# Splitting three output stores of a matmul kernel unevenly over queues and partitions

## The chip, the cores and the metric

The kernel runs on one core of one Trainium2 chip. The metric is the device time of one execution in microseconds (us), as the median of several runs. The core has TensorE for matrix products, VectorE, ScalarE and GpSimd for element work, SyncE for issuing transfers, and 16 DMA engines that move data between device memory (DRAM) and the on-chip memory SBUF, whose 128 rows are called partitions. A DMA is issued by one engine's queue; its data are spread over DMA engines, and each of these adds one step to a semaphore when its share has landed. A full count is 16.

## What is computed

```python
def setup_inputs():
    batch, m, k, n = 16, 512, 1024, 768
    return {
        "x": np.random.randn(batch, m, k).astype(np.float32),
        "weight": np.random.randn(k, n).astype(np.float32),
        "sub_value": np.random.randn(batch, m, n).astype(np.float32),
    }

def reference(x, weight, sub_value):
    return (np.matmul(x, weight) - sub_value).astype(np.float32)
```

The 16 x 512 rows are taken as one matrix of 8192 rows, cut into 64 "m tiles" of 128 rows. `x` has 33.6 MB, `weight` 3.1 MB, `sub_value` and the output 25.2 MB each: 87 MB in all.

## The kernel before

Everything that goes to or from DRAM is issued by SyncE in one fixed order. In the list, `x` is a load of x, `w` one of the weights, `s` one of sub_value, and `o` a store of the output; the numbers are the first m tile and how many.

```python
SEGMENTS = [(at, 8) for at in range(0, 64, 8)]
NX, NSO = 16, 32
TRANSFERS = [
    ('x', 0, 1), ('w', 0, 1), ('x', 1, 1), ('w', 1, 1), ('x', 2, 1), ('w', 2, 1),
    # ... cut ...
    ('o', 8, 8), ('o', 16, 8), ('s', 40, 8), ('x', 48, 8), ('s', 48, 8), ('x', 56, 8),
    ('o', 24, 8), ('o', 32, 8), ('s', 56, 8), ('o', 40, 8), ('o', 48, 8), ('o', 56, 5),
    ('o', 61, 2), ('o', 63, 1),
]
```

The m tiles of one segment (8 of them, 1024 rows) are interleaved over the partitions, so that partition p holds rows 8p to 8p+7 of the segment. A transfer of n m tiles is then, for each partition, one contiguous piece of DRAM of n x 3072 bytes (n x 4096 for x):

```python
    def view(flat, at, n):
        first, size = next(one for one in SEGMENTS if one[0] <= at < sum(one))
        assert at + n <= first + size
        rows = flat[first * P : (first + size) * P].rearrange("(p j) c -> p j c", p=P, j=size)
        return rows[:, at - first : at - first + n]
```

sub_value is loaded into a ring of 32 slots, `so_ring`. The result is written over it in place and stored from there. A store waits for the subtraction of its last m tile (`finish`), a load of sub_value for the store that frees its slots:

```python
            need, by = {
                "w": (set(), "o"),
                "x": ({t for t in old if t >= 0}, "cast"),
                "s": ({t for t in old if t >= 0}, "o"),
                "o": (span, "finish"),
            }[kind]
            # ... cut ...
            here = ring[:, at % size : at % size + n]
            there = view(flat, at, n)
            # ... cut: waits ...
            sem, value = lane((kind, at))
            for t in span:
                landed[kind, t] = (sem, value)
                {"x": of_x, "s": of_s, "o": of_o}[kind][t] = (kind, at)
            if kind == "o":
                here, there = there, here
            sp.add(lambda here=here, there=there: nc.sync.dma_start(out=here, in_=there), waits, (sem, 16))
```

ScalarE rounds x to half precision (`cast`), TensorE (or, for some m tiles, VectorE) transposes it, and TensorE multiplies it with the resident weights; for each m tile there are 8 steps along k, each with two halves of 384 columns. VectorE subtracts:

```python
    def finish(mi):
        assert mi in done["s"]
        done["finish"].add(mi)
        o = so_ring[:, mi % NSO].rearrange("p (h n) -> p h n", h=2)
        po = po_b[:, slot["po", mi]]
        dve.add(lambda: nc.vector.tensor_tensor(
            out=o, in0=po[:, :, :NS], in1=o, op=mybir.AluOpType.subtract
        ), [landed["s", mi], (counter["mul"], mul_at[mi])], count("finish"))
        finish_at[mi] = so_far["finish"]
        issue()
```

At the end SyncE waits for all semaphores of transfers that nothing has waited for yet, closes the program's section, and waits for the last m tile's store:

```python
    left = [one for one in lanes if not one["tags"] <= known]
    last = next(one for one in left if of_o[n_mt - 1] in one["tags"])
    for one in left:
        if one is not last:
            nc.sync.wait_ge(one["sem"], one["value"])
    section.close()
    with tc.tile_critical(sync_engine=mybir.EngineType.SP, no_gpsimd_drain=True):
        nc.sync.wait_ge(last["sem"], last["value"])
```

GpSimd clears three small buffers near the start and does nothing after that.

Of the kernel before, what the change touches and what calls it, by code (L numbers as in the profile page):

```python
# [8 lines left out]
P = 128  # L9
# [5 lines left out]
NX, NSO = 16, 32  # L15
# [16 lines left out]
    ('s', 4, 4), ('x', 12, 4), ('s', 8, 8), ('x', 16, 2), ('x', 18, 6), ('s', 16, 8),  # L32
    ('x', 24, 8), ('o', 0, 8), ('s', 24, 8), ('x', 32, 8), ('s', 32, 8), ('x', 40, 8),
    ('o', 8, 8), ('o', 16, 8), ('s', 40, 8), ('x', 48, 8), ('s', 48, 8), ('x', 56, 8),
    ('o', 24, 8), ('o', 32, 8), ('s', 56, 8), ('o', 40, 8), ('o', 48, 8), ('o', 56, 5),
    ('o', 61, 2), ('o', 63, 1),
]


class Queue:  # L40
# [65 lines left out]
def kernel(  # L106
# [7 lines left out]
    nc = tc.nc  # L114
# [3 lines left out]
    out_flat = out.flatten_outer_dims()  # L118

    M_TOT, K = x_flat.shape  # L120
    _, N = weight.shape
    n_mt = M_TOT // P
# [5 lines left out]
# [6 lines that stand above are left out]
# [6 lines left out]
    def sbuf(name, shape, dtype):  # L140
        return ctx.enter_context(nc.sbuf_tensor(name, shape, dtype)).ap()
# [11 lines left out]
    so_ring = sbuf("so_ring", [P, NSO, N], F32)  # L153
# [11 lines left out]
    counter = {}  # L165
# [4 lines left out]
    def count(name):  # L170
        so_far[name] += 1
        return (counter[name], 1)

    sp, pe = Queue(nc, nc.sync), Queue(nc, nc.tensor)
    act, dve, pool = Queue(nc, nc.scalar), Queue(nc, nc.vector), Queue(nc, nc.gpsimd)
# [6 lines left out]
        out=along, data0=ones, data1=ones, initial=0.0, op0=mybir.AluOpType.mult, op1=mybir.AluOpType.add,  # L182
    ), waits=[(counter["ident"], 1)], then=count("ident"))
    dve.add(lambda: nc.vector.transpose(across, along), waits=[(counter["ident"], 3)], then=count("ident"))  # L184
    for a in range(P // Q):
        here = slice(a * Q, (a + 1) * Q)
        dve.add(lambda here=here: nc.vector.tensor_tensor(  # L187
            out=ident[here, here], in0=along[here], in1=across[here], op=mybir.AluOpType.is_equal,
# [16 lines left out]
    landed = {}  # L205
    cast_at, evac_at, pair_at, turn_at, mul_at, finish_at, w_at = {}, {}, {}, {}, {}, {}, {}
# [16 lines left out]
    done = {"w": set(), "x": set(), "s": set(), "o": set(), "cast": set(), "finish": set()}  # L223
    staged = {}
    lanes = []
    of_x, of_s, of_o = {}, {}, {}
    known = set()

    def lane(tag):

        for one in lanes:
            if one["tags"] <= known:
                break
        else:
            one = {"sem": tc.alloc_semaphore(f"lane{len(lanes)}"), "value": 0, "tags": set()}
            lanes.append(one)
        one["value"] += 16
        one["tags"].add(tag)
        return one["sem"], one["value"]

    def issue():
        nonlocal known
        while todo:
            kind, at, n = todo[0]
            span = set(range(at, at + n))
            old = {t - NX if kind == "x" else t - NSO for t in span}
            need, by = {
                "w": (set(), "o"),
                "x": ({t for t in old if t >= 0}, "cast"),
                "s": ({t for t in old if t >= 0}, "o"),  # L250
                "o": (span, "finish"),
            }[kind]
            if not need <= done[by]:
                return
            todo.pop(0)
            done[kind] |= span
            if kind == "w":

                first = NSO - 2 * (n_c - at)
                st = so_ring[:, first : first + 2]  # L260
                sem, value = lane((kind, at))
                sp.add(lambda st=st, at=at: nc.sync.dma_start(out=st, in_=w_c[at]), then=(sem, 16))  # L262
                for r in range(2):
                    dve.add(
                        lambda at=at, r=r, st=st: nc.vector.tensor_copy(out=w_sb[:, at, r], in_=st[:, r]),  # L265
                        waits=[(sem, value)], then=count("w"),
                    )
                    staged[first + r] = so_far["w"]
                w_at[at] = so_far["w"]
                continue  # L270
            ring, size, flat = {
                "x": (x_ring, NX, x_flat), "s": (so_ring, NSO, sub_flat), "o": (so_ring, NSO, out_flat)
# [3 lines that stand above are left out]
            waits = []  # L276
            if kind == "x" and need:
                waits.append((counter["cast"], max(cast_at[t] for t in need)))
                last = max(need, key=lambda t: cast_at[t])
                known |= {tag for t, tag in of_x.items() if t in cast_at and cast_at[t] <= cast_at[last]}  # L280
            if kind == "s":
                for t in need:
                    waits.append(landed["o", t])
                    known.add(of_o[t])
                for t in span:
                    if t % NSO in staged:
                        waits.append((counter["w"], staged.pop(t % NSO)))
                        known |= {("w", c) for c in w_at if w_at[c] <= waits[-1][1]}
            if kind == "o":
                waits.append((counter["finish"], max(finish_at[t] for t in need)))  # L290
                known |= {of_s[t] for t in finish_at if finish_at[t] <= max(finish_at[u] for u in need)}
            sem, value = lane((kind, at))
            for t in span:
                landed[kind, t] = (sem, value)
                {"x": of_x, "s": of_s, "o": of_o}[kind][t] = (kind, at)
            if kind == "o":
                here, there = there, here
            sp.add(lambda here=here, there=there: nc.sync.dma_start(out=here, in_=there), waits, (sem, 16))  # L298

    def cast(mi):  # L300
        assert mi in done["x"]
        done["cast"].add(mi)
        x_in = x_ring[:, mi % NX]
        first = mi - mi % 2
        waits = [landed["x", mi]]
        if first in ON_DVE:
            if mi == first:
                b, before = take("x16p", N16P, mi)
                if before is not None:
                    waits.append((counter["pair"], pair_at[before]))  # L310
            to = x16p_b[:, slot["x16p", first], mi - first]
        else:
            b, before = take("x16", N16, mi)
            if before is not None:
                waits.append((counter["turn"], turn_at[before]))
            to = x16_b[:, b]
        act.add(lambda: nc.scalar.copy(out=to, in_=x_in), waits, count("cast"))  # L317
        cast_at[mi] = so_far["cast"]
        issue()
# [92 lines left out]
# [14 lines that stand above are left out]
# [59 lines left out]
    for mi in range(HEAD + (EARLY is not None), n_mt):  # L485
# [3 lines left out]
        t = mi + TA  # L489
# [32 lines left out]
    for one in left:  # L522
        if one is not last:
            nc.sync.wait_ge(one["sem"], one["value"])
    section.close()
    with tc.tile_critical(sync_engine=mybir.EngineType.SP, no_gpsimd_drain=True):
        nc.sync.wait_ge(last["sem"], last["value"])
# [30 lines left out]
```

## Time and profile before

| | us |
|---|---|
| device time, median of 3 runs (lowest to highest) | 210.52 (210.41 to 210.6) |
| span of the profiled run, first to last instruction | 208.6 |
| TensorE busy | 195.2 |
| VectorE busy | 128.2 |
| ScalarE busy | 109.0 |
| GpSimd busy | 1.0 |
| last subtraction starts | 201.68 |
| last store issued | 202.66 |

The span in the profile starts with the first instruction and is a little shorter than the device time. In the profile's lines PE is TensorE, DVE is VectorE, ACT is ScalarE, POOL is GpSimd and SPq is SyncE's sequencer, which issues the transfers. "L198" is a line of the kernel. A row of digits gives the busy share in tenths in 40 equal slices of the stretch that was asked for; "DMA" is the mean over the 16 DMA engines. A row of a transfer ends in its size and the median time from its issue to its landing, that is, to the last of its 16 semaphore steps. q1 is the queue of all transfers of data, and q8 and q14 carry instructions to the engines.

### The profile page before, as it was taken

What the parts mean: (1) busy time and instruction counts of PE and PEld (TensorE: products, weight loads), DVE (VectorE), ACT (ScalarE), POOL (GpSimd) and SP (SyncE); (2) the same over time, 40 slices, a digit from 0 to 9 for tenths busy, and PEclk for the clock granted to TensorE, in tenths of its full rate; (3) what the DMA queues carried; (4) which work ended last, traced back from release to release, by engine and by line L of the source; (5) the groups of instructions that cost most, each with busy time, mean ns of one, the idle gap of its engine ahead of it and who ended that gap; (6) DMA issues with size and microseconds to landing.
All of it is one profiled execution on the core that took longest, in us unless ns stands there. A gap on an engine that the chain in (4) does not pass through costs nothing.

```text
span 208.6 us, 2612 instructions
## 1 busy us (share of the span) xinstructions
PE 195.2 (94%) x1234; PEld 75.5 (36%) x700; DVE 128.2 (61%) x224; ACT 109.0 (52%) x113; POOL 1.0 (0%) x7
## 2 busy tenths in 40 slices
PE   6999799969999999999999999999999999999960
PEld 0233243324434433443443443343344344334410
DVE  2323224975993795598399379469739938952330
ACT  3655759506673761944745576183564737507300
POOL 1000000000000000000000000000000000000000
PEclk9999999999999999999999999999999999999997
DMA  6999999999999999999999999999999999999993
GB/s 204 421 427 434 441 424 434 445 429 424 434 448 452 366 443 424 459 415 418 449 440 424 419 429 443 423 470 393 434 463 401 441 424 429 438 443 419 419 422 135
DMA packets 5476, 87.08 MB, mean 417 GB/s; under 512 B 608, under 2 KB 608, under 8 KB 1888
## 3 DMA queue, kind: packets, MB, share of 16 engines
q1 hardware_dynamic: 5472, 87.03, 97.9%
q8 instruction: 1, 0.02, 0.0%
q14 instruction: 3, 0.02, 0.0%
HBM read 61.87 MB, written 25.17 MB: 417 GB/s over the span
## 4 chain that ended last, share of the span: by engine, by line
PE 75%; DMA 13%; DVE 6%; SPq 3%; issue 1%; DVEq 0%
PE po_b L198 67%; DMA so_ring<-in_sub_value_dram 13%; PE pt_b L335 8%; DVE xtp_b L368 3%; DVE so_ring L417 2%; SPq L298 2%; SPq L262 1%; SPq L553 0%; DVEq L59 0%; SPq L138 0%
## 5 line engine op out<-in xcount | busy, mean ns | idle before, releaser
L198 PE MATMUL po_b<-w_sb,xt_b 128*128 128x384 f16 x704 | 126.0, 326 | 1.2 <-DVE w_sb L265 0.9
L417 DVE TENSOR_TENSOR so_ring<-po_b,so_ring 128x768 f32<-128x768 f32 x64 | 60.8, 957 | 59.3 <-PE po_b L198 39.9
L348 ACT COPY xt_b<-pt_b 128x1024 f16<-128x1024 f16 x44 | 44.5, 1012 | 65.3 <-PE pt_b L335 64.3
L368 DVE STREAM_TRANSPOSE xtp_b<-x16p_b 32x256 f32<-32x256 f32 x144 | 62.7, 435 | 2.3
L198 PE MATMUL po_b<-w_sb,xtp_b 128*128 128x384 f16 x320 | 61.3, 326 | 1.9 <-DVE xtp_b L368 1.7
L397 PEld LDWEIGHTS <-xt_b 128*128 128x128 f16 x352 | 34.4, 98 | 58.9 <-issue 55.6
L317 ACT CAST x_b<-x_ring 128x1024 f16<-128x1024 f32 x46 | 47.2, 1048 | 5.0 <-DMA x_ring<-in_x_dram 4.9
L335 PE MATMUL pt_b<-ident,x_b 128*128 128x128 f32 x184 | 47.5, 274 | 1.7 <-ACT x_b L317 1.7
L335 PEld LDWEIGHTS pt_b<-ident,x_b 128*128 128x128 f32 x184 | 25.4, 141 | 44.6 <-issue 36.8
L317 ACT CAST x16p_b<-x_ring 128x1024 f16<-128x1024 f32 x18 | 18.8, 1046 | 14.9 <-DMA x_ring<-in_x_dram 14.9
L397 PEld LDWEIGHTS <-xtp_b 128*128 128x128 f16 x160 | 15.7, 98 | 20.4 <-issue 18.3
L265 DVE CAST w_sb<-so_ring 128x768 f16<-128x768 f32 x8 | 4.1, 556 | 11.6 <-DMA so_ring<-in_weight_dram 11.6
L198 PE MATMUL po_b<-idle_x,idle_w 128*128 128x512 f16 x26 | 7.7, 448 | 1.7 <-POOL idle_x L178 1.7
L348 ACT COPY xtp_b<-pt_b 128x1024 f16<-128x1024 f16 x2 | 2.0, 1012 | 2.5 <-PE pt_b L335 2.5
L317 ACT ACT_TABLE_LOAD x1 | 1.3, 1283 | 0.9 <-SPq L138 0.9
L427 PEld LDWEIGHTS <-idle_w 128*128 128x128 f16 x4 | 0.4, 99 | 1.7 <-POOL idle_x L178 1.7
L187 DVE TENSOR_TENSOR ident<-along,across 32x32 f32<-32x32 f32 x4 | 0.7, 183 | 0.1
L179 DVE MEMSET ones<- 128x32 f32 x1 | 0.1, 85 | 1.0 <-SPq L138 1.0
L178 POOL MEMSET idle_x<- 128x512 f16 x1 | 0.5, 528 | 0.0
L499 ACT CAST stub<-ident 128x1 f16<-128x1 f32 x2 | 0.4, 194 | 0.0
L184 DVE STREAM_TRANSPOSE across<-along 128x32 f32<-128x32 f32 x1 | 0.2, 212 | 0.0
L476 POOL MEMSET mark<- 128x1 f32 x1 | 0.1, 98 | 23.7 <-ACT xtp_b L348 23.7
(7 smaller groups left out, 1.0 us busy)
## 6 DMA issues: line engine op xcount, KB each, us to landing
so_ring<-in_sub_value_dram SPq DMA_DIRECT2D x7, 3072.0 KB, 24.2
out_dram<-so_ring SPq DMA_DIRECT2D x7, 3072.0 KB, 26.6
x_ring<-in_x_dram SPq DMA_DIRECT2D x5, 4096.0 KB, 23.1
x_ring<-in_x_dram SPq DMA_DIRECT2D x2, 2048.0 KB, 27.2
so_ring<-in_weight_dram SPq DMA_DIRECT2D x4, 768.0 KB, 8.3
x_ring<-in_x_dram SPq DMA_DIRECT2D x1, 3072.0 KB, 28.8
x_ring<-in_x_dram SPq DMA_DIRECT2D x2, 1024.0 KB, 24.8
out_dram<-so_ring SPq DMA_DIRECT2D x1, 1920.0 KB, 10.2
```

What stands on the lines that cost most here:

```text
L178: pool.add(lambda: nc.gpsimd.memset(idle_x, 0.0), then=count("idle"))
L187: dve.add(lambda here=here: nc.vector.tensor_tensor(out=ident[here, here], in0=along[here], in1=across[here], op=mybir.AluOpType.is_equal, ...
L198: return nc.tensor.add_instruction(mybir.InstMatmult(name=nc.get_next_instruction_name(), engine=full.engine, ins=list(full.ins), outs=lis ...
L262: sp.add(lambda st=st, at=at: nc.sync.dma_start(out=st, in_=w_c[at]), then=(sem, 16))
L265: lambda at=at, r=r, st=st: nc.vector.tensor_copy(out=w_sb[:, at, r], in_=st[:, r]),
L298: sp.add(lambda here=here, there=there: nc.sync.dma_start(out=here, in_=there), waits, (sem, 16))
L317: act.add(lambda: nc.scalar.copy(out=to, in_=x_in), waits, count("cast"))
L335: pe.add(lambda: nc.tensor.transpose(words, from_, ident), waits, count("turn") if last else None)
L348: act.add(lambda: nc.scalar.copy(out=to, in_=pt_b[:, b]), waits, count("evac"))
L368: dve.add(lambda: nc.vector.transpose(xt[b * Q : (b + 1) * Q, :, a * Q : (a + 1) * Q], x16[a * Q : (a + 1) * Q, :, b * Q : (b + 1) * Q],), ...
L397: pe.add(lambda weights=weights: nc.tensor.ldweights(weights, tile_position=(0, 0)), [w for w in waits if w[0] in ready])
L417: dve.add(lambda: nc.vector.tensor_tensor(out=o, in0=po[:, :, :NS], in1=o, op=mybir.AluOpType.subtract), [landed["s", mi], (counter["mul"] ...
```

## The change

The store of m tiles 40 to 47 is cut: SyncE stores 40 to 45, and GpSimd's own queue stores 46 and 47, in three transfers of 5, 112 and 11 partitions, once they are computed and the last load of sub_value has landed. The store of m tiles 61 and 62 stays with SyncE but goes out as two transfers, of partitions 0 to 119 and 120 to 127. The same bytes are stored to the same places. [...] the change is a way to give the 16 DMA engines unequal shares of these stores. Each GpSimd transfer has a semaphore of its own, for which SyncE waits at the close.

```diff
--- before.py
+++ after.py
@@ -32,9 +32,11 @@
     ('s', 4, 4), ('x', 12, 4), ('s', 8, 8), ('x', 16, 2), ('x', 18, 6), ('s', 16, 8),
     ('x', 24, 8), ('o', 0, 8), ('s', 24, 8), ('x', 32, 8), ('s', 32, 8), ('x', 40, 8),
     ('o', 8, 8), ('o', 16, 8), ('s', 40, 8), ('x', 48, 8), ('s', 48, 8), ('x', 56, 8),
-    ('o', 24, 8), ('o', 32, 8), ('s', 56, 8), ('o', 40, 8), ('o', 48, 8), ('o', 56, 5),
+    ('o', 24, 8), ('o', 32, 8), ('s', 56, 8), ('o', 40, 6), ('q', 46, 2), ('o', 48, 8), ('o', 56, 5),
     ('o', 61, 2), ('o', 63, 1),
 ]
+OWN = (112, 117), (0, 112), (117, 128)
+SPLIT = {61: ((0, 120), (120, 128))}
 
 
 class Queue:
@@ -225,6 +227,7 @@
     lanes = []
     of_x, of_s, of_o = {}, {}, {}
     known = set()
+    own = []
 
     def lane(tag):
 
@@ -249,11 +252,21 @@
                 "x": ({t for t in old if t >= 0}, "cast"),
                 "s": ({t for t in old if t >= 0}, "o"),
                 "o": (span, "finish"),
+                "q": (span, "finish"),
             }[kind]
             if not need <= done[by]:
                 return
             todo.pop(0)
-            done[kind] |= span
+            done["o" if kind == "q" else kind] |= span
+            if kind == "q":
+                here, there = so_ring[:, at % NSO : at % NSO + n], view(out_flat, at, n)
+                waits = [(counter["finish"], max(finish_at[t] for t in need)), landed["s", n_mt - 1]]
+                for low, high in OWN:
+                    own.append(tc.alloc_semaphore(f"own{low}"))
+                    pool.add(lambda low=low, high=high, here=here, there=there: nc.gpsimd.dma_start(
+                        out=there[low:high], in_=here[low:high], max_dma_last_dim=4 * N,
+                    ), waits, (own[-1], 16))
+                continue
             if kind == "w":
 
                 first = NSO - 2 * (n_c - at)
@@ -289,13 +302,16 @@
             if kind == "o":
                 waits.append((counter["finish"], max(finish_at[t] for t in need)))
                 known |= {of_s[t] for t in finish_at if finish_at[t] <= max(finish_at[u] for u in need)}
-            sem, value = lane((kind, at))
+            if kind == "o":
+                here, there = there, here
+            for low, high in SPLIT.get(at, ((0, P),)) if kind == "o" else ((0, P),):
+                sem, value = lane((kind, at))
+                sp.add(lambda here=here[low:high], there=there[low:high]: nc.sync.dma_start(
+                    out=here, in_=there
+                ), waits, (sem, 16))
             for t in span:
                 landed[kind, t] = (sem, value)
                 {"x": of_x, "s": of_s, "o": of_o}[kind][t] = (kind, at)
-            if kind == "o":
-                here, there = there, here
-            sp.add(lambda here=here, there=there: nc.sync.dma_start(out=here, in_=there), waits, (sem, 16))
 
     def cast(mi):
         assert mi in done["x"]
@@ -522,6 +538,8 @@
     for one in left:
         if one is not last:
             nc.sync.wait_ge(one["sem"], one["value"])
+    for sem in own:
+        nc.sync.wait_ge(sem, 16)
     section.close()
     with tc.tile_critical(sync_engine=mybir.EngineType.SP, no_gpsimd_drain=True):
         nc.sync.wait_ge(last["sem"], last["value"])
```

## The prediction

> **What bounds the kernel now.** I read three views in this order. First the page's top: busy shares, slices and DMA queues.
>
> ```profile
> PE 195.2 (94%) x1234; PEld 75.5 (36%) x700; DVE 128.2 (61%) x224; ACT 109.0 (52%) x113; POOL 1.0 (0%) x7
> ...
> DMA  6999999999999999999999999999999999999993
> ...
> q1 hardware_dynamic: 5472, 87.03, 97.9%
> ```
>
> Two resources are full: TensorE at 94%, and the 16 DMA engines at 97.9% with one queue. GpSimd has nothing to do. To see which of the two ends last I read the timeline of the end, and then the DMA issues of its last windows.
>
> ```profile
> 196.28 5.36 PE L198 MATMUL po_b<-w_sb,xt_b 128*128 128x384 f16 x32
> ...
> 201.68 0.96 DVE L417 TENSOR_TENSOR so_ring<-po_b,so_ring 128x768 f32<-128x768 f32 x1 [1.64 <-PE po_b L198]
> ...
> out_dram<-so_ring SPq DMA_DIRECT2D x1, 1920.0 KB, 10.2
> ...
> out_dram<-so_ring SPq DMA_DIRECT2D x1, 768.0 KB, 6.3
> ...
> out_dram<-so_ring SPq DMA_DIRECT2D x1, 384.0 KB, 4.6
> ```
>
> TensorE ends at 201.64 us, the last subtraction at 202.64. The last three stores (m tiles 56-60, 61-62, 63) are issued at 194.32, 200.06 and 202.66, so with these latencies they land at 204.5, 206.4 and 207.3. They lie in a queue behind each other: 0.94 us between the last two landings is just the time for the last 24.6 KB of each engine. So the DMA sets the end, but is it all 16 engines? The DMA view of 204.3 to 207.3 us answers:
>
> ```profile
> DMA  8969969433421321321312112112021011000000
> GB/s 369 492 246 451 369 246 369 205 123 123 164 82 82 164 82 82 164 82 41 123 41 82 41 41 82 41 41 82 0 82 41 0 41 41 0 0 0 0 0 0
> ```
>
> Each slice is 0.075 us. Full rate ends in the seventh slice, near 204.85; then for two microseconds only a few engines still work. Each store raises its semaphore by 16, one step for an engine, and the trace has the 16 times of the last store. Relative to their median (205.31 us) they are, in us:
>
> ```
> -0.45 -0.43 -0.21 -0.19 -0.18 -0.06 -0.02 -0.01 0.01 0.02 0.05 0.19 0.78 1.17 1.66 1.98
> ```
>
> Four engines are late, call them D (0.78), C (1.17), B (1.66) and A (1.98). Read for earlier transfers, the last two are +0.35 and +0.39 at 28.95 us, then A jumps to 1.50 (a 16 KB packet of the instruction queue q8 runs at 30.9 us), and to 2.06 by 74 us; B jumps from 0.83 to 1.78 when an 8 KB instruction packet of q14 runs at 146.0 us. The debts stay to the end, since every transfer gives each engine equal shares. The mean of the 16 numbers is 0.27: perfect sharing would end at 205.58 instead of 207.29. **The most that any rebalancing can win is thus 1.7 us, 0.8%.** TensorE would not forbid it: the fastest engine has the last tile out at 204.86.
>
> [...]
>
> **The change part by part.**
>
> *m tiles 61 and 62 in 120 and 8 partitions.* A partition's piece is 2 x 3072 B = 6144 B, and packets of that size last 234 ns here. [...] 8 x 234 = 1.87 us. That is nearly A's debt, 1.98, and I choose to believe that the split was sized for it[...]. [...] A then ends at 1.98 - 1.87 = +0.11, and **B becomes the end**: 1.66 [...], 1.89 [...]. Gain 0.32 or 0.09 us. One more issue on SyncE (0.33 us, like the others) puts m tile 63's store at most 0.4 us later, 203.1; A's queue is done with nearly everything by then, but B's is full until 206, so nothing shows.
>
> *m tiles 46 and 47 on GpSimd's queue.* Removed: a quarter of the 3072 KB store issued at 171.27, whose packets of 24576 B last 912 ns. They become 18432 B (0.75 x 912 = 684) and, at one tile row a packet as the kernel limits them, two of 3072 B spaced 117 ns apart: 684 + 234 = 918, +6 ns, times 8 partitions +0.05 us for each engine. The semaphore writes (9 ns each, up to three more) add 0.03. GpSimd waits for the last s load, 170.88 + 14.5 = 185.4 us, so that no load is delayed. By then it has been idle for 160 us; [...] the data are out well before SyncE's backlog ends at 204. What it does to the debts depends on the engines chosen. [...]
>
> *The close.* SyncE waits for m tile 61's landing (206.35), runs 0.8 us of its closing sequence, and then finds m tile 63 landed within 0.13 us. Waits go two to an instruction, 0.065 us apiece, so four more semaphores cost up to 0.13 us and just use up this slack; half of it, 0.07, is charged.
>
> *Sum*, central case: -0.32 (A out of the way, B at the end) + 0.08 (smaller packets and semaphores) + 0.07 (close) = -0.17 us. To this I add a quarter of a chance that B is relieved as well, which brings the end to C: 1.98 - 1.17 = 0.81, less 0.15 = -0.66. Weighted, about -0.3: 210.52 - 0.3 = **210.2 us**.
>
> **Rivals.**
> 1. *The wrong engine.* [...] Time: +0.15 to +0.4, 210.7 to 210.9. For it: no row of the profile names the engines. Against: 1.87 against 1.98 is too good a fit for chance.
> 2. *GpSimd's queue costs.* [...] could add 0.2 to 0.6 us on every engine: 210.6 to 211.0. For it: the DMA is full, so any bubble counts. Against: what it carries is 786 KB of 87 MB, 17 us before the end[...].
> 3. *The debts arise anew.* Another instruction layout changes where the instruction packets fall, and with them who is late: either way by the 0.3 to 1.0 us of one such jump.
> 4. *Both late engines relieved*, down to the limit of 1.7 us less 0.15: 209.0 to 209.7. For it: the odd 5, 112 and 11 are hard to explain as an even split.
>
> **Range and chances.** The three runs of before lie within 0.2 us, so the range comes from the rivals: 209.5 (most of rival 4) to 210.8 (rival 1 or 2 with middle sizes). Two per cent is 4.2 us. The gain is bounded at 1.7 us, and a loss of 4.2 needs a stall that nothing here hints at[...]: 0.01 for faster, 0.97 same, 0.02 slower.
>
> **What would show it.** Right: the store of 120 partitions raises its semaphore from 15 engines, one of the late increments vanishes from the last store's 16, and the low tail of the DMA slices after 204.85 gets shorter by 0.3 us or more, while TensorE still ends near 201.6. The three GpSimd transfers land before 200. Wrong: the last increment of the last store stays 1.9 us or more behind the median (rival 1), the median itself moves later by 0.2 or more (rival 2), or the late engines are others than the q8 and q14 jumps made (rival 3). The prediction as a whole fails if TensorE or the loads move, which would mean that GpSimd's transfers start before the last load has landed.

## The result, and the profile after

The changed kernel takes 212.81 us (212.11 to 213.25, four runs) against 210.56 before: ratio 1.0104, 95% interval 1.0075 to 1.0133. Measured once more beside the experiments, the ratio is 1.0105 (1.0079 to 1.0131). It is 2.2 us slower, where 0.3 us less had been predicted; 212.81 lies above the range.

The top of the page after, the same lines as were shown of before, and the queue that is new:

```profile
PE 196.3 (93%) x1234; PEld 75.5 (36%) x700; DVE 128.3 (61%) x224; ACT 108.8 (52%) x113; POOL 2.9 (1%) x10
...
DMA  6999999999999999999999999999999999999981
...
q1 hardware_dynamic: 5479, 86.25, 96.2%
q0 software_dynamic: 192, 0.79, 1.0%
```

The arithmetic engines and the bytes are about as before; 0.79 MB have moved to GpSimd's queue q0. Its three transfers land at 192.85, 200.38 and 201.58 us, two of them after the 200 that the prediction had named as a sign of being right. The last load of sub_value lands at 185.34 us (185.35 before). The timeline of the end:

```profile
196.39 5.36 PE L200 MATMUL po_b<-w_sb,xt_b 128*128 128x384 f16 x32
...
200.18 3.96 SPq L309 DMA_DIRECT2D out_dram<-so_ring  x3
201.79 0.96 DVE L433 TENSOR_TENSOR so_ring<-po_b,so_ring 128x768 f32<-128x768 f32 x1 [1.64 <-PE po_b L200]
```

TensorE ends at 201.75 (201.64 before), the last subtraction 0.11 us later than before. So all but 0.11 us of the difference comes after the arithmetic. The DMA view of 204.3 to 207.3 us, where before the row thinned out from its seventh slice on:

```profile
DMA  9692995299286599839948955972753126022021
GB/s 328 246 410 82 451 451 205 82 328 328 123 328 246 246 410 574 328 123 451 410 164 328 451 205 205 369 287 82 246 205 123 41 82 164 0 82 82 0 82 41
```

Most engines are now at work until about 206.5, and a few beyond the view's end. The last store's 16 semaphore steps, relative to their median, which is now 206.82 instead of 205.31 us:

```
-0.69 -0.63 -0.61 -0.34 -0.24 -0.24 -0.11 -0.08 0.08 0.14 0.17 0.19 0.40 0.93 0.94 2.81
```

The last landing moved from 207.29 to 209.63, by 2.34 us: 1.51 by which **all engines are later**, and 0.83 by which **the latest is further behind** (2.81 against 1.98). Both had been predicted to fall or stay.

Why are all engines later? The busy times by stretches of 1 us show it; the last two numbers of a row are the mean busy share of the DMA engines and GB/s. Before, and then after:

```profile
202.00:203.00 1.00, 0.00 (x0) 0.00 (x0) 0.64 (x1) 0.00 (x0) 0.00 (x0) 1.00 0.92 387
203.00:204.00 1.00, 0.00 (x0) 0.00 (x0) 0.00 (x0) 0.00 (x0) 0.00 (x0) 1.00 0.98 409
```

```profile
202.00:203.00 1.00, 0.00 (x0) 0.00 (x0) 0.75 (x1) 0.00 (x0) 0.00 (x0) 1.00 1.02 347
203.00:204.00 1.00, 0.00 (x0) 0.00 (x0) 0.00 (x0) 0.00 (x0) 0.00 (x0) 1.00 0.93 255
204.00:205.00 1.00, 0.00 (x0) 0.00 (x0) 0.00 (x0) 0.00 (x0) 0.00 (x0) 1.00 0.78 270
```

Read share and rate together. From 203 to 204 the engines are busy for 0.93 of the time, nearly as before, and move 255 GB/s instead of 409. They hardly wait for work: **many packets take longer**. The packets' records agree. Before, a packet of 6144 B never lasts over 236 ns after 186 us; after, up to 854 ns, and those of 15360 B up to 1593 instead of 573 to 596. Added up over all packets that start after 186 us, the time beyond the usual durations (121, 234, 573, 686 and 912 ns for 3072, 6144, 15360, 18432 and 24576 B) is 15.8 engine-us, 0.99 us for each of the 16 engines; before it is 0.5, or 0.03.

A second thing stands out in the issues. SyncE's issue of the store of m tile 63, before and after (duration in ns after "x1:"):

```profile
L298 SPq DMA_DIRECT2D out_dram<-so_ring x1: 332/332/332, 202.7 to 202.7; - x1
```

```profile
L309 SPq DMA_DIRECT2D out_dram<-so_ring x1: 1362/1362/1362, 202.8 to 202.8; - x1
```

The issue of the 8 partitions before it takes 1466 ns. Is that the cause, or only another sign of crowded DMA engines? The experiments had to tell.

### The profile page after: what moved, and what is told of

It is laid out like the page before. It is cut to its first block, busy times and chain, and to the rows that moved or that the text cites. A ratio compares the mean times of both kernels' runs of the same rounds, so it can differ in the third digit from the quotient of the medians.

```text
span 211.1 us, 2619 instructions
## 1 busy us (share of the span) xinstructions
PE 196.3 (93%) x1234; PEld 75.5 (36%) x700; DVE 128.3 (61%) x224; ACT 108.8 (52%) x113; POOL 2.9 (1%) x10
## 4 chain that ended last, share of the span: by engine, by line
PE 74%; DMA 13%; DVE 5%; SPq 3%; issue 1%; DVEq 0%
PE po_b L200 67%; DMA so_ring<-in_sub_value_dram 13%; PE pt_b L351 7%; DVE xtp_b L384 3%; DVE so_ring L433 2%; SPq L309 2%; SPq L275 1%; SPq L571 0%; DVEq L61 0%; SPq L140 0%
## 5 line engine op out<-in xcount | busy, mean ns | idle before, releaser
L200 PE MATMUL po_b<-idle_x,idle_w 128*128 128x512 f16 x26 | 9.0, 507 | 1.7 <-POOL idle_x L180 1.7
L266 POOL DMA_DIRECT2D out_dram<-so_ring x3 | 1.9, 649 | 160.0 <-DMA so_ring<-in_sub_value_dram 160.0
```

What stands on the lines that cost most here:

```text
L200: return nc.tensor.add_instruction(mybir.InstMatmult(name=nc.get_next_instruction_name(), engine=full.engine, ins=list(full.ins), outs=lis ...
L266: pool.add(lambda low=low, high=high, here=here, there=there: nc.gpsimd.dma_start(out=there[low:high], in_=here[low:high], max_dma_last_di ...
```

## Experiments

Theory **P**, a conjecture of mine: in a transfer cut by partitions, DMA engines collide on partitions, and packets last longer. Rivals: **G**, GpSimd's queue costs; **I**, late or slow issues cost. All edits are against the changed kernel; "no q" stands for the line that gives m tiles 40 to 47 back to SyncE whole:

```diff
-('o', 40, 6), ('q', 46, 2),
+('o', 40, 8),
```

### The halves of the change by themselves

The change cuts two stores, that of m tiles 40 to 47 and that of 61 and 62. Here each cut is made without the other.

**split_only**: no q.

> Only the store of m tiles 61 and 62 is split (120 and 8 partitions); m tiles 40 to 47 are stored by SyncE in one transfer as before. Theory P (partitions: [...] packets of 6144 B last up to 600 ns instead of 234): 212.0 to 212.5 us, the last store's median near 206.6 and the latest engine still 2.5 us or more behind it. Theory G (GpSimd's queue is what costs): 210.3 to 210.6. Theory I (the additional issue and the unusual number of engines hold SyncE up, so the last store comes late): 212 as well, but with packets of normal length and gaps between them.

Ratio 1.0022 (1.0002 to 1.0043), far less than P expected. **q_only**:

```diff
-SPLIT = {61: ((0, 120), (120, 128))}
+SPLIT = {}
```

> Only m tiles 46 and 47 go by GpSimd's queue in 5, 112 and 11 partitions; the store of 61 and 62 is whole. Theory P: 210.6 to 210.9 us [...]. Theory G: 212.0 to 212.5. Theory I: 210.5 to 210.7.

Ratio 1.0015 (1.0002 to 1.0027). No theory had this right as a whole: each half costs 0.3 to 0.5 us, the two together 2.2. The stretched packets behave in the same way: 7.4 engine-us with the split alone, 2.6 with GpSimd's transfers alone, 15.8 with both. With the split alone the row of 203 to 204 us shows the mark of P, weaker:

```profile
203.00:204.00 1.00, 0.00 (x0) 0.00 (x0) 0.00 (x0) 0.00 (x0) 0.00 (x0) 1.00 0.82 313
```

**two_halves**: no q, and

```diff
+SPLIT = {61: ((0, 64), (64, 128))}
```

> m tiles 61 and 62 are stored in partitions 0 to 63 and 64 to 127[...]. No GpSimd store. Theory P: slower by 1 to 2 us, 211.5 to 212.5, with packets of 6144 B well over 234 ns. Theory I: at most 0.4 us slower (one more issue[...]), packets 234 ns. Theory G: 210.5.

Ratio 1.0016 (1.0006 to 1.0027), with packets of 6144 B up to 1045 ns. So it doesn't take pieces as uneven as 120 and 8. P has the packets right and the time too high.

**two_tiles**: no q, no cut by partitions, and

```diff
-('o', 61, 2), ('o', 63, 1),
+('o', 61, 1), ('o', 62, 1), ('o', 63, 1),
```

> The control for the number of transfers: m tile 61 and m tile 62 in a transfer of 128 partitions each; no GpSimd store. Theory P and theory G: 210.4 to 210.7 us, nothing changes. Theory I: 210.8 to 211.5, since SyncE has one issue more in the same place as the split has.

Ratio 0.9993 (0.9982 to 1.0004), no packet stretched. One more issue costs nothing; theory I in its simple form falls. Against two_halves, this run moves the same bytes in as many transfers and differs in the direction of the cut (and with it in packets of 3072 instead of 6144 B, and in an earlier issue of m tile 61): 0.5 engine-us of stretched packets for the cut by columns, 8.3 for the cut by partitions.

### What makes the two act together

**after_again**: the changed kernel unaltered.

> The changed kernel unaltered, beside the others. Alone its two halves cost 0.46 us (split) and 0.3 us (GpSimd's queue), together 2.2. If this is a real interaction, it is again 212 to 213.3 us, the issues of the 8-partition store and of m tile 63 last over 1 us instead of 0.33, and the latest engine is 2.5 us or more behind the median of the last store. If the sum was an accident of the first measurement: 210.8 to 211.5.

It is real (1.0105), with issues of 1162 and 1157 ns and 17.5 engine-us of stretched packets.

**q_whole_split**: GpSimd in one whole transfer.

```diff
-OWN = (112, 117), (0, 112), (117, 128)
+OWN = ((0, 128),)
```

> As the changed kernel, but GpSimd stores m tiles 46 and 47 in one transfer of 128 partitions. Theory S (a second queue is enough: its packets leave the late engine later still when the 120 and 8 partitions come): 212 to 213 us. Theory U (it is the uneven 5, 112 and 11 that put the late engine back): 210.8 to 211.3, as with the split alone.

Ratio 1.0032 (1.0014 to 1.0050), hardly more than the split alone, with 5.5 engine-us: theory U, that the uneven cut matters.

**sp46_split**: SyncE stores 46 and 47.

```diff
-('q', 46, 2),
+('o', 46, 2),
```

> As the changed kernel, but SyncE stores m tiles 46 and 47, in one transfer of 128 partitions after that of 40 to 45; nothing goes by GpSimd. Both theories S and U: 210.7 to 211.2 us, as with the split alone. If the cutting of the store of 40 to 47 is what matters: 212 or more.

Ratio 1.0021 (1.0013 to 1.0029), the split's cost.

**q_low8**:

```diff
-SPLIT = {61: ((0, 120), (120, 128))}
+SPLIT = {61: ((0, 8), (8, 128))}
```

> As the changed kernel, but m tiles 61 and 62 are cut into partitions 0 to 7 and 8 to 127: the same numbers of engines and of transfers. Theory P (which partitions the eight engines crowd on decides who is put back): the latest engine's packets of 15360 B, up to 1593 ns in the changed kernel, are back near 573 and it is 2.1 us behind the median at most; 210.9 to 211.7 us. If only the number of engines and transfers matters: 212 to 213.

Ratio 1.0098 (1.0079 to 1.0118); packets of 15360 B still reach 1621 ns. Which eight partitions go separately doesn't matter; my form of P, that those eight put the late engine back, was too narrow.

**q_early**: GpSimd's transfers don't wait for the last load.

```diff
-waits = [(counter["finish"], max(finish_at[t] for t in need)), landed["s", n_mt - 1]]
+waits = [(counter["finish"], max(finish_at[t] for t in need))]
```

> As the changed kernel, but GpSimd's three transfers don't wait for the last load of sub_value: they go out when m tile 47 is computed, near 158 us instead of 186. Theory O (overlap: GpSimd's packets must still be under way when the cut store of 61 and 62 is issued): 210.8 to 211.5 us, SyncE's last issues take 0.3 to 0.5 us. Theory L (the three uneven transfers leave something behind that slows later issues, however early they were): 212 to 213.5, issues of over 1 us.

Ratio 1.0215 (1.0173 to 1.0257): both times missed. The last load of sub_value lands at 189.84 us instead of 185.35, the subtractions with it, and the last store is issued at 208.11 instead of 202.66. The issues take 413, 293 and 360 ns, as theory O said. Yet the packets of 6144 B after 186 us are stretched by 18.2 engine-us in all, more than in any other run, though none lasts over 738 ns: stretched packets come without slow issues.

Why is the load late? GpSimd's 0.79 MB now go out ahead of it, and the store in front of it lands 2.1 us later at the median engine (178.44 us, 176.35 before). The median engine then takes 1.5 us longer for the load itself, and packets are stretched again: from 174 to 186 us the packets of 24576 B exceed 912 ns by 26.5 engine-us, the longest with 2475 ns; before it is 0.3. The rows of 182 to 186 us, before and in q_early:

```profile
182.00:186.00 4.00, 4.00 (x28) 1.46 (x14) 1.50 (x4) 0.18 (x2) 0.00 (x0) 1.00 1.03 442
```

```profile
182.00:186.00 4.00, 4.00 (x28) 1.38 (x14) 1.10 (x3) 0.34 (x2) 0.00 (x0) 1.00 0.99 310
```

GpSimd's last packet had ended at 173.42 us, and the load and the stores beside it use all 128 partitions. So packets can also be stretched while no cut transfer is under way; what stretches these is not shown.

**q_three_whole**: three whole GpSimd transfers, each with a semaphore of its own.

```diff
-('o', 40, 6), ('q', 46, 2),
+('o', 40, 5), ('q', 45, 1), ('q', 46, 1), ('q', 47, 1),
-OWN = (112, 117), (0, 112), (117, 128)
+OWN = ((0, 128),)
```

> As the changed kernel, but GpSimd stores m tiles 45, 46 and 47 in one whole transfer of 128 partitions each: three transfers, none uneven. If the number of GpSimd's transfers (three against one) makes SyncE's issues slow: 212 to 213 us. If it is that they are uneven: 211.2 to 211.8, as with one whole transfer.

Ratio 1.0045 (1.0030 to 1.0061). The number of GpSimd's transfers is not it.

**q_112_16**:

```diff
-OWN = (112, 117), (0, 112), (117, 128)
+OWN = (0, 112), (112, 128)
```

> As the changed kernel, but GpSimd cuts m tiles 46 and 47 into 112 and 16 partitions[...]. If the numbers 5 and 11 matter (engines without data in them): 211.2 to 211.8 us. If any cut of the partitions does: 212 to 213.

Ratio 1.0125 (1.0080 to 1.0170). The numbers 5 and 11 aren't it either: this cut by partitions on GpSimd's side does the same.

**q_two_tiles**: GpSimd as in the change, two_tiles on SyncE.

> GpSimd's 5, 112 and 11 as in the changed kernel, and m tiles 61 and 62 in a whole transfer each: as many issues by SyncE as in the changed kernel, but all for 16 engines. If one more issue behind GpSimd's is enough for the interaction: 212 to 213 us, issues of over 1 us. If it takes the 120 and 8 partitions: 210.6 to 211.1, issues of 0.33 us.

Ratio 1.0027 (1.0012 to 1.0042), 2.7 engine-us. **q_halves**: GpSimd as in the change, two_halves on SyncE.

> As the changed kernel, but m tiles 61 and 62 are cut into 64 and 64 partitions[...]. If the interaction needs transfers of SyncE with fewer than 16 engines: 210.9 to 211.3 us, issues up to 0.7 us as without GpSimd. If it needs only that both queues cut the partitions: 212 to 213, issues of over 1 us.

Ratio 1.0081 (1.0057 to 1.0106), 14.3 engine-us, an issue of 2316 ns. So the two act together when **both queues cut by partitions**, whether SyncE's two pieces are equal or, as in the changed kernel (15.8 engine-us), not. They do it without meeting: in the changed kernel GpSimd's last packet of data ends at 199.74 us, and the first packet of the cut store of 61 and 62 starts at 202.05. So GpSimd's cut seems to leave something behind that the later store runs into; what it is was not found.

**last_by_scalar**: the store of m tile 63 from ScalarE's queue.

```diff
+by, own_q = (nc.scalar, act) if kind == "o" and at == 63 else (nc.sync, sp)
-sp.add(lambda here=here[low:high], ...: nc.sync.dma_start(
+own_q.add(lambda here=here[low:high], ..., by=by: by.dma_start(
```

> The changed kernel, with the store of m tile 63 issued by ScalarE's queue; everything else by SyncE and GpSimd as there. If what is held up is SyncE's own queue, ScalarE's issue takes 0.4 us and the median of the last store falls back by 0.5 us or more to about 206.2, while the latest engine stays: 212.0 to 212.8 us. If the hold-up is in what all queues share, the issue takes over 1 us here as well: 212.5 to 213.3.

Ratio 1.0131 (1.0108 to 1.0153). Here are the issue, from the records of the store's tile, and the row of 203 to 204 us:

```profile
L310 ACTq DMA_DIRECT2D out_dram<-so_ring x1: 369/369/369, 202.5 to 202.5; - x1
...
DMA to landing us min/median/max: 7.4/7.4/7.4
```

```profile
203.00:204.00 1.00, 0.00 (x0) 0.00 (x0) 0.00 (x0) 0.00 (x0) 0.00 (x0) 1.00 0.96 246
```

ScalarE issues in 0.37 us and a full microsecond before SyncE's issue ended in the changed kernel, but the store lands after 7.4 us and its median step is at 206.87, against 206.82. Nothing is gained. The slow issue of this store is a sign, not the cause; the engines are busy (0.96) at 246 GB/s.

### Which engine is late, and where the engines meet

**mid_120**: the same cut on an earlier store of SyncE's, with plenty queued behind. The expectation sets two cases apart: the latest engine is the one that the 120 partitions leave out, as the prediction took it, or it is another.

```diff
-('q', 46, 2),
+('o', 46, 2),
-SPLIT = {61: ((0, 120), (120, 128))}
+SPLIT = {46: ((0, 120), (120, 128))}
```

> No GpSimd store and no cut of 61 and 62; instead SyncE stores m tiles 46 and 47 in 120 and 8 partitions, with 3072 KB and more queued behind, so that no late issue can show. [...] its step in the last store comes down from 2.0 us behind the median to about 0. If it is another, a middle engine goes 1.9 us ahead of the median instead and the last stays 2.0 or more behind. Theory P: the 120 partitions still collide, 210.7 to 211.5 us; if only issues count: 210.4 to 210.7.

Ratio 1.0133 (1.0113 to 1.0152), dearer than at the end and over what either theory said. The 16 steps of the store of 48 to 55, which follows, relative to their median:

```
-1.43 -0.44 -0.38 -0.32 -0.25 -0.23 -0.14 -0.11 0.11 0.12 0.45 0.49 0.57 1.29 3.04 4.26
```

One engine gained (-1.43). I take it for the one that the cut store left out, whose 120 partitions gave 15 steps by landing. It isn't the latest: that one stood at 2.23 in the load before these stores and is now at 4.26; the second went from 1.27 to 3.04. The median engine took 1.96 us for the cut store, near the 1.87 of 8 pieces. So **those who pay are the late engines**. They are still storing m tiles 40 to 45 while the others are already at the cut store: a packet of 18432 B takes 1142 ns instead of 686, and the latest falls to 2.88 behind. Then it takes 3.48 us for its share of the cut store (191.87 to 195.35 us), while the others are already at the store of 48 to 55.

```profile
DMA  9967994235210402111201102101010000100000
```

In this kernel's DMA view of 204.3 to 210 us one or two engines hold the end up for about 3 us.

**mid_104**:

```diff
+SPLIT = {46: ((0, 104), (104, 128))}
```

> As mid_120, but m tiles 46 and 47 go out in 104 and 24 partitions[...]. If [...] a debt can be moved to other engines, the last step falls to 1.7 us or less behind the median and the time to 210.1 to 210.4. If [...] the partitions that the others now read for it hold it up: 210.8 to 211.8, the last 2.0 or more behind.

Ratio 1.0095 (1.0075 to 1.0114). In the store after it three engines are 1.89 to 2.24 us ahead, those that the 104 partitions, with 13 steps by landing, left out, and the latest is 3.20 behind. It took a share of the 24 partitions (0.78 us more) and in mid_120 none of the 8. Which of the 16 engines it is, no trace shows.

**mid_120_apart**: the cut store behind that of 48 to 55.

```diff
-('o', 46, 2), ('o', 48, 8), ('o', 56, 5),
+('o', 48, 8), ('o', 46, 2), ('o', 56, 5),
```

> As mid_120, but the cut store of m tiles 46 and 47 is issued after the whole store of 48 to 55 instead of before it, so that the late engines, when the cut store runs, are still storing another segment: the same SBUF partitions, but other rows of DRAM, not the neighbours in the same 24 KB piece. If the collisions are in SBUF (two engines on the same partitions): as mid_120, the latest engine 4 us behind the median, 212.8 to 213.5 us. If they are in DRAM (neighbouring rows): the latest engine 2.0 to 2.8 us behind, 210.6 to 211.5.

Ratio 1.0103 (1.0083 to 1.0123), 212.60 us: the latest engine falls from 2.44 to 4.16 behind although it is storing another segment, with other rows of DRAM. That fits engines meeting in the same SBUF partitions, and not neighbouring rows; other ways to meet in DRAM weren't excluded.

## Why the prediction was wrong

**The bound, the debts and the limit** held. TensorE and the loads didn't move, the end is the latest DMA engine, and no rebalancing found here gains anything. The transfer of 120 partitions gave 15 steps by landing, from 204.26 to 208.69 us, and one at once, at 200.71.

**"1.98 - 1.87 = +0.11", the relief of the latest engine, failed.** It rested on the choice that A is the engine that the 120 partitions leave out, because 1.87 fitted 1.98. The fit was chance. After the change A's steps in the last three stores are at 206.33, 208.69 and 209.63 us: 2.36 us for a full share of the 120, none of the 8, a full share of the last. So A is not the engine that the 120 leave out. In mid_120 and mid_104 the latest engine isn't among those left out either. Rival 1 named this, but at 0.15 to 0.4 us. Which engines GpSimd's 5, 112 and 11 partitions spare is shown by no trace either: the quarter of a chance for B was an estimate of mine.

**"8 x 234 = 1.87 us" and "684 + 234 = 918, +6 ns" are the terms that made the loss.** They priced a cut transfer by its bytes, with durations from whole transfers. (GpSimd's pieces went out as one packet of 6144 B each, not as two of 3072; at the usual 234 ns that comes to the same.) Where +0.08 us for each engine was charged for smaller packets and semaphores, the stretching alone measures 0.96 (0.99 less 0.03 before). The remaining 0.55 of the 1.51 by which the median moved isn't resolved: it includes what the engines stood idle from 204 to 206, where their share is 0.78 and 0.84 in the rows by stretches. The step from 1.98 to 2.81 fits the same thing on the latest engine: packets of 15360 B, which late engines are still storing then, last up to 1593 ns.

**The parts were added up**, and that was wrong too. GpSimd's queue alone and the split alone cost 0.15% and 0.22%; both cutting by partitions cost 1.04%. A reading that suggests itself is that GpSimd's packets put the engines further out of step (up to 2.59 us behind in the store of 48 to 55, against 2.00 before), and that engines out of step meet others on their partitions. The record doesn't bear it out. The lag of the latest engine in that store doesn't tell dear runs from cheap ones: it is 2.60 us in q_whole_split and 3.13 in q_only, which cost 0.32% and 0.15%. And in q_early the engines entered the cut store within 0.1 us of each other but for two, and still had stretched packets. Why two cuts cost more than their sum stays open.

**The close** was about right: from the last landing to the end of the span 1.45 us against 1.30, +0.15 where 0.07 was charged.

That engines collide on partitions is argued and not seen, since no record names a packet's engine or its partitions, and where two would meet is not settled. What is measured is the difference: for m tiles 61 and 62 the median engine took 2.34 us in two_halves and 1.88 in two_tiles. Its cause is shown by no run.

## What to carry to other kernels

Store all 128 partitions in one transfer and cut along the columns when a store must be split: here a cut by columns cost nothing (two_tiles, ratio 0.9993). A single cut by partitions cost 0.3 to 0.5 us in the last store but one or on GpSimd's queue, but 2.0 to 2.8 us in SyncE's queue with more stores behind it (mid_104, mid_120), and two cuts on two queues cost 2.2 us. A late DMA engine has to be identified, by transfers that leave engines out, before anything is moved away from it; a sum that fits is no identification. And when transfers get slower, look at busy share and GB/s together: here a full share at a fallen rate meant stretched packets, and an earlier issue of the last store did not help.

## What was new about the hardware

- SyncE's transfers of 120 and 8 partitions in the changed kernel, and of 104 and 24 in mid_104, raised their semaphores in 15, 8, 13 and 12 steps by landing, and with one further step at once.
- GpSimd's three transfers in the changed kernel moved one packet of 6144 B for each of their 128 partitions. There were 16 more packets of 8 B: 11 from 190.45 us on, with the 5 partitions, and 5 from 197.64 us on. The semaphore of each transfer took 16 steps.
- In the kernel before, an instruction packet of 16 KB and one of 8 KB coincide with jumps of 1.1 and 0.95 us in one engine's debt each, which stays to the end. A cut store with more behind it fell on the late engines: mid_120 nearly doubled the debt of the latest, 2.23 to 4.26 us. In two_halves, by contrast, the latest came closer to the median, 2.14 to 1.60 us.
- Packets of one size took up to 3.6 times their usual time (854 against 234 ns in the changed kernel) while the engines stayed busy: 255 GB/s at a share of 0.93 from 203 to 204 us, against 409 at 0.98 before. There, busy DMA engines did not move data at their usual rate.
